# Gated linear attention on TensorE: one head per 32-row strip and PSUM bank in place of block-diagonal queries

## The chip, the cores and the metric

The program runs on one core of one Trainium2 chip, in one launch. The metric is the device time of an execution in microseconds (us). An engine is TensorE (PE, with its weight loads listed apart as PEld), VectorE (DVE), ScalarE (ACT), GpSimd (POOL) or SyncE (SP, which issues most transfers).

## The reference, cut to what matters

The program is a decoder trunk of two layers over 512 tokens. Each layer mixes three groups of heads, adds the result to the stream and runs a feed-forward network. The change touches one of the three groups, the gated linear attention with 4 heads of 32 key and 64 value channels:

```python
def step(state, inp):
    qc, kc, vc, gc = inp
    bcum = jnp.cumsum(gc, axis=2)
    o_inter = jnp.einsum('bhck,bhkv->bhcv', qc * jnp.exp(bcum), state)
    diff = bcum[:, :, :, None, :] - bcum[:, :, None, :, :]
    decay = jnp.exp(jnp.where(causal[None, None, :, :, None], diff, -jnp.inf))
    attn = jnp.einsum('bhik,bhjk,bhijk->bhij', qc, kc, decay)
    o_intra = jnp.einsum('bhij,bhjv->bhiv', attn, vc)
    ...
```

For each pair of a query i and an earlier key j in a chunk, the product of query and key is weighted in each of the 32 key channels by its own decay. The state carries the earlier chunks.

## The kernel before

Tokens stand in 4 chunks of 128. Channels of queries and keys stand on the 128 partitions: head h has partitions 32h to 32h+31 (`qkT[0]` queries, `qkT[1]` keys, 128 x 512 each).

The decay between i and j is split at a point between them, so that it becomes a factor of the query times a factor of the key. A chunk has 7 levels for this, with blocks of 64, 32, 16, 8, 4, 2 and 1 tokens (`LEVELS`). At each level, half of the chunk's tokens (64) act as queries and the other half as keys. The loop of lines 737 to 794 does for each chunk `t`:

- Lines 740 to 744: TensorE sums the log decays (`ghl` by the 0/1 matrix `tsel`) into PSUM in three pieces of 512, 512 and 128 columns. ScalarE takes the exponential into `E`, 9 planes of 128 tokens: one for each level, one for the state's update and one for its readout.
- Lines 745 to 747: ScalarE copies each head's queries into a block-diagonal tile `qbd`, whose other blocks are zero (line 730). The four heads lie side by side in its columns.
- Lines 751 to 762: VectorE multiplies `qbd` by each level's plane into `xq` (line 760, 4 heads x 64 queries = 256 columns, one instruction for each level). It multiplies four planes at a time by the keys (line 761), in place; these are the keys `xk`.
- Lines 764 to 765: VectorE writes the diagonal into `at`, the chunk's attention matrix.
- Lines 766 to 772: for each level, one matmul of all 128 rows: the weights are `xk` (128 x 128), 256 columns of `xq` stream past. Since `qbd` is zero outside of a head's own rows, each head's columns get its own product. VectorE then copies the allowed entries from PSUM into `at` under a mask (line 772). Two PSUM banks ("t") take turns.
- Lines 773 to 794: TensorE multiplies the state (line 777) and `at` (line 779) with their values into bank "o"; the keys are transposed (line 784), multiplied with the values (line 788) and added to the state `sbd`.

PSUM has 8 banks of 512 columns. The function `psum(tag)` (line 141) takes a tile of one bank from a pool with a fixed number for each tag: g 2, s 3, t 2, o 1. Which of a tag's banks a tile gets, and what it waits for, is settled by the planner of the language when it lays out the program. The planner also fixes the order of each engine's instructions, from its estimates of when each is ready and from the order in the source. So matmuls of the next projection, site "B" (line 834, through the helper `mm3` at lines 286 to 288, into banks "g"), stand between those of the loop in TensorE's queue. Each engine works through its queue in that order.

A matmul on float32 operands appears in the trace as two loads and two matmul records; a split operand (`hl`, `kt`, type fp32r) as one of each.

Of the kernel before, what the change touches and what calls it, by code (L numbers as in the profile page):

```python
# [10 lines left out]
F32 = mybir.dt.float32  # L11
# [5 lines left out]
ALU = mybir.AluOpType  # L17
AX = mybir.AxisListType

P = 128  # L20
# [11 lines left out]
GH = 4  # L32
DK = 32
# [10 lines left out]
XKP = ()  # L44
# [13 lines left out]
LEVELS = (64, 32, 16, 8, 4, 2, 1)  # L58
# [65 lines left out]
def trunk_kernel(ctx: ExitStack, tc: tile.TileContext, a, out):  # L124
    nc = tc.nc
# [6 lines left out]
    pp = ctx.enter_context(tc.tile_pool(name="pp", bufs=1, space=bass.MemoryType.PSUM))  # L132
    uid = [0]

    def nm(s):
        uid[0] += 1
        return f"{s}_{uid[0]}"

    PB = PBK

    def psum(tag):
        return pp.tile([P, 512], F32, tag=tag, name=nm("ps" + tag), bufs=PB[tag])

    def small(n, tag, bufs=4, dt=F32):
        return sm.tile([P, n], dt, tag=tag, name=nm(tag), bufs=bufs)
# [6 lines left out]
    o = 0  # L152
# [186 lines left out]
    with tc.tile_pool(name="x0", bufs=1, reuse_waits="tile") as xp:  # L339
# [8 lines left out]
        for t in range(NT):  # L348
            tk = slice(t * P, (t + 1) * P)
            r = xp.tile([P, D], F32, name=nm("xr"))  # L350
# [4 lines left out]
            for hf in range(2):  # L355
                m4 = slice(4 * hf, 4 * hf + 4)
                ps = psum("s")
# [90 lines left out]
    def mixer(l, norm, xkt, eu=None):  # L448
# [47 lines left out]
        with tc.tile_pool(name=f"mx{l}", bufs=1, reuse_waits="tile") as mp:  # L496
# [13 lines left out]
            with tc.tile_pool(name=f"ma{l}", bufs=1, reuse_waits="tile") as ap:  # L510
# [45 lines left out]
                for t in range(NT):  # L556
                    v = uv[:, t, 256:512]
                    nc.vector.tensor_scalar(v, v, vmean[:, t : t + 1], None, op0=ALU.subtract)
                    s = tmp(256)
# [5 lines left out]
                for t in range(NT):  # L565
                    v = uv[:, t, 256:512]
# [81 lines left out]
            with tc.tile_pool(name=f"mg{l}", bufs=1, reuse_waits="tile") as gp:  # L648
# [77 lines left out]
                nc.vector.tensor_copy(diag, dps[:, 0:16].rearrange("p (t h) -> p t h", t=NT))  # L726
                osb = mp.tile([P, NT, 256], F32, tag="PT", name=nm("osb"), bufs=3)
                sbd = gp.tile([P, 256], F32, name=nm("sbd"))
                qbd = gp.tile([P, GH, P], F32, name=nm("qbd"))
                nc.gpsimd.memset(qbd, 0.0)  # L730
                ats = []
                for n in range(2):
                    at_ = gp.tile([P, GH, P], F32, name=nm("at"))
# [3 lines left out]
                for t in range(NT):  # L737
                    tk = slice(t * P, (t + 1) * P)
                    E = gp.tile([P, 9, P], F32, tag="E", name=nm("E"), bufs=2)
                    for c0, c1 in ((0, 4), (4, 8), (8, 9)):  # L740
                        ps = psum("s")[:, 0 : (c1 - c0) * P]
                        nc.tensor.matmul(ps, ghl[:, 0, tk], tsel[:, c0 * P : c1 * P], start=True, stop=False)
                        nc.tensor.matmul(ps, ghl[:, 1, tk], tsel[:, c0 * P : c1 * P], start=False, stop=True)
                        nc.scalar.activation(E[:, c0:c1, :].rearrange("p l i -> p (l i)"), ps, AF.Exp, scale=1.0 / 16)
                    for h in range(GH):
                        r = slice(32 * h, 32 * h + 32)
                        nc.scalar.copy(qbd[r, h, :], qkT[0][r, tk])

                    xqs = []
                    xk = E[:, 0:8, :]  # L750
                    for l0, l1 in ((0, 4), (4, 8)):
                        for lv in range(l0, min(l1, 7)):
                            s = LEVELS[lv]
                            nb = 64 // s
                            xq = gp.tile([P, GH, 64], F32, tag="xq", name=nm("xq"), bufs=4)
                            xqs.append(xq)
                            ev = E[:, lv, :].rearrange("p (b u s) -> p b u s", u=2, s=s)[:, :, 1, :]
                            qv = qbd.rearrange("p h (b u s) -> p h b u s", u=2, s=s)[:, :, :, 1, :]
                            xv = xq.rearrange("p h (b s) -> p h b s", s=s)
                            nc.vector.tensor_tensor(xv, qv, ev.unsqueeze(1).to_broadcast([P, GH, nb, s]), op=ALU.mult)  # L760
                        (nc.gpsimd if l0 // 4 in XKP else nc.vector).tensor_tensor(xk[:, l0:l1], xk[:, l0:l1],
                                                qkT[1][:, tk].unsqueeze(1).to_broadcast([P, l1 - l0, P]), op=ALU.mult)
                    at = ats[t % 2]
                    nc.vector.copy_predicated(at, eye8.unsqueeze(1).to_broadcast([P, GH, P]),
                                              diag[:, t, :].unsqueeze(2).to_broadcast([P, GH, P]))
                    for lv, s in enumerate(LEVELS):
                        nb = 64 // s
                        ps = psum("t")[:, 0:256]
                        nc.tensor.matmul(ps, xk[:, lv, :], xqs[lv].rearrange("p h i -> p (h i)"), start=True, stop=True)
                        av = at.rearrange("p h (b u s) -> p h b u s", u=2, s=s)[:, :, :, 1, :]  # L770
                        mv = lmask[:, lv, :].rearrange("p (b s) -> p b s", s=s).unsqueeze(1).to_broadcast([P, GH, nb, s])
                        nc.vector.copy_predicated(av, mv, ps.rearrange("p (h b s) -> p h b s", h=GH, s=s))
                    ops = psum("o")[:, 0:256]
                    if t > 0:
                        xi = tmp(P)
# [4 lines left out]
                                         start=t == 0, stop=t == 0 or h == GH - 1)  # L780
                    nc.scalar.copy(osb[:, t, :], ops)
                    if t < NT - 1:
                        kps = psum("t")[:, 0:P]
                        nc.tensor.transpose(kps, xk[:, 7, :], ident)
                        ktok = tmp(P)
                        nc.scalar.copy(ktok, kps)
                        sps = psum("t")[:, 0:256]
                        nc.tensor.matmul(sps, ktok, gv[:, t, :], start=True, stop=True)
                        if t == 0:
                            nc.vector.tensor_tensor(sbd, sps, bdm, op=ALU.mult)  # L790
                        else:
                            sm_ = tmp(256)
                            nc.vector.tensor_tensor(sm_, sps, bdm, op=ALU.mult)
                            nc.vector.scalar_tensor_tensor(sbd, sbd, E[:, 8, 127:128], sm_, op0=ALU.mult, op1=ALU.add)
# [620 lines left out]
```

## Time and profile before

| what | us |
|---|---|
| median of 3 runs | 1343.45 |
| lowest and highest of them | 1343.28, 1351.97 |
| the profiled execution's own time | 1343.64 |
| its span, first to last instruction | 1341.9 |

The profiled execution lies 0.19 us above the median. Its time is 1.7 us more than its span. In the rows below, "x" is the number of instructions of a group, a duration is that of the record (matmul records overlap, since the engine starts one while the one before drains), and idle time follows with what ended it.

### The profile page before, as it was taken

To read this page: it belongs to the slowest core of one execution; us is meant where nothing else is said; L and a number is where in the kernel's file an instruction comes from. 1 tells how busy PE (TensorE), PEld (TensorE's weight loads), DVE (VectorE), ACT (ScalarE), POOL (GpSimd) and SP (SyncE) were. 2 spreads that over 40 slices of the span, in tenths; PEclk is the share of its full clock that TensorE was granted. 3 is DMA by queue.
4 is the path that set the end of the run, shared out by engine and by line. 5 is a ranking of instruction groups with operands and counts; after the bars stand their busy time and mean duration, and the time that the engine had idled before them with its cause. 6 is when DMAs were issued, how large, how long until landed. Compare 5 with 4: busy or idle time off the path is not lost.

```text
span 1341.9 us, 17478 instructions
## 1 busy us (share of the span) xinstructions
PE 1298.7 (97%) x6434; PEld 1054.7 (79%) x6434; DVE 949.1 (71%) x1661; ACT 624.5 (47%) x1164; POOL 176.4 (13%) x158
## 2 busy tenths in 40 slices
PE   6999999999999999999999999999999999999997
PEld 5888776777888888888888877767788888888785
DVE  5636889997865785586644498999778457736775
ACT  6344336665542543254442632667544435514532
POOL 2111021114000100010312102111220001000103
PEclk9999999999999999999999999999999999999999
DMA  8521131006335785384363302201343348754721
GB/s 280 156 81 48 32 95 32 17 17 159 109 99 121 206 213 152 105 203 111 96 181 97 91 21 63 79 17 33 91 129 95 110 120 205 225 126 126 195 88 64
DMA packets 128554, 150.41 MB, mean 112 GB/s; under 512 B 9034, under 2 KB 82516, under 8 KB 128468
## 3 DMA queue, kind: packets, MB, share of 16 engines
q1 hardware_dynamic: 115504, 128.31, 31.5%
q0 software_dynamic: 8704, 16.78, 7.4%
q10 hardware_dynamic: 4260, 4.20, 1.1%
q8 instruction: 51, 0.84, 0.3%
q14 instruction: 35, 0.29, 0.1%
HBM read 147.17 MB, written 2.10 MB: 111 GB/s over the span
## 4 chain that ended last, share of the span: by engine, by line
PE 77%; DVE 12%; ACT 4%; DMA 3%; issue 3%; POOL 1%; SPq 0%; ACTq 0%; DVEq 0%; POOLq 0%
PE psg L286 10%; PE psg L287 10%; PE psg L288 10%; PE pss L286 4%; PE pst L286 4%; PE pss L288 4%; PE pss L287 4%; PE pst L288 4%; PE pst L287 4%; PE pso L593 2%; DVE hl L274 2%; PE pst L1010 2%; PE pso L288 2%; PE pso L286 2%; PE pso L287 2%
## 5 line engine op out<-in xcount | busy, mean ns | idle before, releaser
L271 ACT CAST hl<-raw 128x1024 fp32r<-128x1024 f32 (+3 forms) x170 | 175.6, 1034 | 224.3 <-PE pst L288 66.2
L274 DVE TENSOR_TENSOR hl<-raw,hl 128x1024 fp32r<-128x1024 f32 (+3 forms) x170 | 207.8, 1223 | 100.3 <-ACT hl L271 97.5
L286 PE MATMUL psg<-hl,kt 128*128 128x512 f32 (+2 forms) x480 | 179.4, 375 | 4.1 <-ACT hl L271 2.1
L288 PE MATMUL psg<-hl,kt 128*128 128x512 f32 (+2 forms) x480 | 178.2, 372 | 0.0
L287 PE MATMUL psg<-hl,kt 128*128 128x512 f32 (+2 forms) x480 | 177.3, 370 | 0.0
L286 PEld LDWEIGHTS psg<-hl,kt 128*128 128x128 f32 x480 | 91.1, 190 | 19.0 <-DVE gqk L698 2.7
L288 PEld LDWEIGHTS psg<-hl,kt 128*128 128x128 f32 x480 | 91.1, 190 | 12.9
L287 PEld LDWEIGHTS psg<-hl,kt 128*128 128x128 f32 x480 | 91.0, 189 | 12.8
L287 PE MATMUL psg<-kt,hl 128*128 128x512 f32 x248 | 99.6, 402 | 1.2 <-DVE kt L249 1.2
L286 PE MATMUL psg<-kt,hl 128*128 128x512 f32 x248 | 99.6, 403 | 0.0
L288 PE MATMUL psg<-kt,hl 128*128 128x512 f32 x248 | 98.3, 398 | 0.0
L271 ACT CAST hl<-wx 128x1024 fp32r<-128x1024 f32 x48 | 50.3, 1049 | 78.6 <-PE pst L288 63.3
L274 DVE TENSOR_TENSOR hl<-wx,hl 128x1024 fp32r<-128x1024 f32 x48 | 58.7, 1223 | 18.0 <-ACT hl L271 17.4
L253 ACT CAST PT<-pst 128x384 fp32r<-128x384 f32 (+1 forms) x96 | 46.7, 519 | 37.9 <-PE pst L1010 37.6
L254 DVE TENSOR_TENSOR PT<-pst,PT 128x384 fp32r<-128x384 f32 (+1 forms) x96 | 54.8, 595 | 10.5 <-ACT PT L253 9.6
L1002 POOL TENSOR_TENSOR P<-P,rr 128x512 f32<-128x512 f32 x32 | 35.5, 1109 | 174.8 <-DVE rr L999 134.3
L1010 PE MATMUL pst<-ident,P 128*128 128x128 f32 x320 | 53.2, 277 | 2.6 <-DVE P L1004 2.6
L287 PEld LDWEIGHTS psg<-kt,hl 128*128 128x128 f32 x248 | 46.9, 189 | 9.9 <-DVE kt L249 2.0
L288 PEld LDWEIGHTS psg<-kt,hl 128*128 128x128 f32 x248 | 46.8, 189 | 8.0
L286 PEld LDWEIGHTS psg<-kt,hl 128*128 128x128 f32 x248 | 46.7, 189 | 7.8 <-ACT kt L253 0.3
L286 PE MATMUL pss<-hl,kt 128*128 128x512 f32 x128 | 50.3, 393 | 1.7 <-DVE ft L1302 1.3
L288 PE MATMUL pss<-hl,kt 128*128 128x512 f32 x128 | 50.0, 390 | 0.0
(442 smaller groups left out, 3139.6 us busy)
## 6 DMA issues: line engine op xcount, KB each, us to landing
raw<-in_w_gate_dram SPq DMA_DIRECT2D x44, 512.0 KB, 3.8
raw<-in_w_up_dram SPq DMA_DIRECT2D x44, 512.0 KB, 4.4
raw<-in_w_in_dram SPq DMA_DIRECT2D x32, 512.0 KB, 3.7
raw<-in_w_down_dram SPq DMA_DIRECT2D x20, 512.0 KB, 3.9
raw<-in_w_down_dram SPq DMA_DIRECT2D x36, 256.0 KB, 4.1
raw<-in_w_out_dram SPq DMA_DIRECT2D x16, 512.0 KB, 4.0
w<-in_cmp_w_k_dram SPq DMA_DIRECT2D x16, 256.0 KB, 5.4
w<-in_cmp_w_v_dram SPq DMA_DIRECT2D x16, 256.0 KB, 3.1
```

The lines of the kernel that those rows point to most:

```text
L253: nc.scalar.copy(hi, src)
L254: nc.vector.tensor_tensor(lo, src, hi.bitcast(F32), op=ALU.subtract)
L271: nc.scalar.copy(hl[:, 0, 0:n], raw[:, 0:n])
L274: e_.tensor_tensor(hl[:, 1, 0:n], raw[:, 0:n], hl[:, 0, 0:n].bitcast(F32), op=ALU.subtract)
L286: nc.tensor.matmul(ps, lh, rh, start=start, stop=False, skip_group_check=skip)
L287: nc.tensor.matmul(ps, lh, rl, start=False, stop=False, skip_group_check=skip)
L288: nc.tensor.matmul(ps, ll, rh, start=False, stop=stop, skip_group_check=skip)
L593: nc.tensor.matmul(ps[:, hh * 65 : (hh + 1) * 65], wu[:, kk, hh * P : (hh + 1) * P], kvS[w_i][:, s % 8, s // 8 : s // 8 + 65], start=s == ...
L1002: nc.gpsimd.tensor_tensor(ps_[i], ps_[i], rr[:, i : i + 1].to_broadcast([P, P * (i + 1)]), op=ALU.mult)
L1010: nc.tensor.transpose(T[:, c : c + P], ps_[i][:, j * P : (j + 1) * P], ident)
```

## The change

- All 8 PSUM banks become one tile, `banks`. `psum(tag)` gives a slice of it; a tag's banks are taken in turn, in the order of the source: g has banks 0 and 1, t 2 and 3, s 4 to 6, o 7.
- `qbd`, its clearing and its four copies for each chunk go. `xq` becomes one tile of 7 levels x 64 queries, and a level's query product has 64 columns in place of 256.
- A level's matmul becomes four, one for each head, on that head's 32 partitions, each with 64 columns into the head's own bank (2 to 5), at column 64 times the level. All 28 matmuls of a chunk come first in the source, then the seven masked copies, from the smallest block to the largest; a copy reads its level's columns of all four banks in one instruction.
- The sums of the log decays, the transposed keys and the state's product all use bank 6.

```diff
+    banks = pp.tile([P, 8, 512], F32, name="banks")
+    first_bank = {"g": 0, "t": 2, "s": 4, "o": 7}
+    taken = {k: 0 for k in first_bank}
     def psum(tag):
-        return pp.tile([P, 512], F32, tag=tag, name=nm("ps" + tag), bufs=PB[tag])
+        taken[tag] += 1
+        return banks[:, first_bank[tag] + (taken[tag] - 1) % PB[tag], :]
...
-                qbd = gp.tile([P, GH, P], F32, name=nm("qbd"))
-                nc.gpsimd.memset(qbd, 0.0)
...
                     for c0, c1 in ((0, 4), (4, 8), (8, 9)):
-                        ps = psum("s")[:, 0 : (c1 - c0) * P]
+                        ps = banks[:, 6, 0 : (c1 - c0) * P]
...
-                    for h in range(GH):
-                        r = slice(32 * h, 32 * h + 32)
-                        nc.scalar.copy(qbd[r, h, :], qkT[0][r, tk])
+                    xq = gp.tile([P, 7, 64], F32, tag="xq", name=nm("xq"), bufs=2)
...
-                            xq = gp.tile([P, GH, 64], F32, tag="xq", name=nm("xq"), bufs=4)
-                            nc.vector.tensor_tensor(xv, qv, ev.unsqueeze(1).to_broadcast([P, GH, nb, s]), op=ALU.mult)
+                            ev, qv = (v.rearrange("p (b u s) -> p b u s", u=2, s=s)[:, :, 1, :] for v in (E[:, lv, :], qkT[0][:, tk]))
+                            nc.vector.tensor_tensor(xq[:, lv, :].rearrange("p (b s) -> p b s", s=s), qv, ev, op=ALU.mult)
...
-                    for lv, s in enumerate(LEVELS):
+                    for lv in range(7):
+                        for h in range(GH):
+                            r = slice(DK * h, DK * h + DK)
+                            nc.tensor.matmul(banks[:, 2 + h, lv * 64 : lv * 64 + 64], xk[r, lv, :], xq[r, lv, :], start=True, stop=True)
+                    for lv in reversed(range(7)):
+                        s = LEVELS[lv]
                         nb = 64 // s
-                        ps = psum("t")[:, 0:256]
-                        nc.tensor.matmul(ps, xk[:, lv, :], xqs[lv].rearrange("p h i -> p (h i)"), start=True, stop=True)
+                        ps = banks[:, 2 : 2 + GH, lv * 64 : lv * 64 + 64]
...
-                        nc.vector.copy_predicated(av, mv, ps.rearrange("p (h b s) -> p h b s", h=GH, s=s))
+                        nc.vector.copy_predicated(av, mv, ps.rearrange("p h (b s) -> p h b s", s=s))
...
-                        kps = psum("t")[:, 0:P]
+                        kps = banks[:, 6, 0:P]
...
-                        sps = psum("t")[:, 0:256]
+                        sps = banks[:, 6, 0:256]
```

## Rows read from the trace of the kernel before

**Rows 1.** The page: the span, and each engine's busy time, share and instructions.

```profile
span 1341.9 us, 17478 instructions
PE 1298.7 (97%) x6434; PEld 1054.7 (79%) x6434; DVE 949.1 (71%) x1661; ACT 624.5 (47%) x1164; POOL 176.4 (13%) x158
```

**Rows 2.** Busy time by stretch: the loop over chunks in layer 0 and layer 1.

```profile
core 0: us, PE busy (x) PEld busy (x) DVE busy (x) ACT busy (x) POOL busy (x), PEclk, DMA share, GB/s
118.70:156.00 37.30, 36.73 (x167) 27.16 (x166) 33.21 (x86) 9.38 (x28) 1.59 (x2) 1.00 0.03 12
774.00:811.00 37.00, 36.43 (x165) 27.28 (x165) 32.83 (x86) 9.37 (x28) 1.59 (x2) 1.00 0.02 9
```

**Rows 3.** Groups by line, TensorE, 118.7 to 156: busy us, mean ns | idle.

```profile
L769 PE MATMUL pst<-xq,E 128*128 128x256 f32 x56 | 16.2, 395 | 0.4 <-DVE E L761 0.3
L286 PE MATMUL psg<-hl,kt 128*128 128x512 f32 x22 | 10.3, 469 | 0.1
L288 PE MATMUL psg<-hl,kt 128*128 128x512 f32 x22 | 9.8, 446 | 0.0
L287 PE MATMUL psg<-hl,kt 128*128 128x512 f32 x22 | 9.5, 430 | 0.0
L779 PE MATMUL pso<-gv,at 128*128 128x64 f32 x24 | 3.1, 272 | 0.1
L788 PE MATMUL pst<-gv,tmp 128*128 128x256 f32 x6 | 2.0, 423 | 0.0
L777 PE MATMUL pso<-sbd,tmp 128*128 128x256 f32 x6 | 1.9, 392 | 0.0
```

**Rows 4.** Timeline of TensorE, start and us: the first and last of nine matmuls.

```profile
95.31 0.39 PE L286 MATMUL psg<-kt,hl 128*128 128x512 f32 x1
...
97.12 0.39 PE L288 MATMUL psg<-kt,hl 128*128 128x512 f32 x1
```

**Rows 5.** Timeline of TensorE's weight loads: full arrays, 256 and 64 columns streamed.

```profile
792.14 0.85 PEld L769 LDWEIGHTS pst<-xq,E 128*128 128x128 f32 x4
...
126.48 0.97 PEld L779 LDWEIGHTS pso<-gv,at 128*128 128x128 f32 x8 [0.52 <-DVE at L772]
```

**Rows 6.** Timeline of TensorE around matmuls that use 17 rows of the array.

```profile
90.83 0.39 PE L287 MATMUL psg<-kt,hl 128*128 128x512 f32 x1
91.14 0.96 PEld L684 LDWEIGHTS pss<-wup,tmp 17*128 17x128 f32 x8 [0.35 <-issue]
...
92.23 0.50 PE L288 MATMUL psg<-kt,hl 128*128 128x512 f32 x1
...
92.57 0.40 PE L286 MATMUL psg<-kt,hl 128*128 128x512 f32 x1
```

**Rows 7.** Groups by line, VectorE, 118.7 to 156.

```profile
L772 DVE COPY_PREDICATED at<-m,pst 128x256 f32<-128x256 uint8 x27 | 13.7, 506 | 0.7 <-PE pst L769 0.5
L760 DVE TENSOR_TENSOR xq<-qbd,E 128x256 f32<-128x256 f32 x24 | 10.3, 430 | 3.1 <-PE pst L769 2.6
L761 DVE TENSOR_TENSOR E<-E,gqk 128x512 f32<-128x512 f32 x8 | 5.5, 685 | 0.1
...
L825 DVE SCALAR_TENSOR_TENSOR tmp<-psg,rstd,cf 128x64 f32<-128x64 f32 x4 | 1.1, 271 | 0.0
...
L776 DVE TENSOR_TENSOR tmp<-E,gqk 128x128 f32<-128x128 f32 x3 | 0.8, 280 | 0.0
```

**Rows 8.** Groups by line, ScalarE, 118.7 to 156.

```profile
L747 ACT COPY qbd<-gqk 32x128 f32<-32x128 f32 x12 | 3.6, 296 | 9.8 <-DVE xq L760 9.6
L744 ACT ACTIVATE E<-pss 128x512 f32<-128x512 f32 x4 | 2.2, 598 | 0.1
```

More of the change, by code (lines that the diff above doesn't have):

```diff
@@ L744, in mixer @@
                         nc.scalar.activation(E[:, c0:c1, :].rearrange("p l i -> p (l i)"), ps, AF.Exp, scale=1.0 / 16)
-                    for h in range(GH):
-                        r = slice(32 * h, 32 * h + 32)
-                        nc.scalar.copy(qbd[r, h, :], qkT[0][r, tk])
-                    xqs = []
+                    xq = gp.tile([P, 7, 64], F32, tag="xq", name=nm("xq"), bufs=2)
                     xk = E[:, 0:8, :]
@@ L753, in mixer @@
                             s = LEVELS[lv]
-                            nb = 64 // s
-                            xq = gp.tile([P, GH, 64], F32, tag="xq", name=nm("xq"), bufs=4)
[L756 to L759, printed above, removed]
-                            nc.vector.tensor_tensor(xv, qv, ev.unsqueeze(1).to_broadcast([P, GH, nb, s]), op=ALU.mult)
-                        (nc.gpsimd if l0 // 4 in XKP else nc.vector).tensor_tensor(xk[:, l0:l1], xk[:, l0:l1],
+                            ev, qv = (v.rearrange("p (b u s) -> p b u s", u=2, s=s)[:, :, 1, :] for v in (E[:, lv, :], qkT[0][:, tk]))
+                            nc.vector.tensor_tensor(xq[:, lv, :].rearrange("p (b s) -> p b s", s=s), qv, ev, op=ALU.mult)
+                        nc.vector.tensor_tensor(xk[:, l0:l1], xk[:, l0:l1],
                                                 qkT[1][:, tk].unsqueeze(1).to_broadcast([P, l1 - l0, P]), op=ALU.mult)
```

## The prediction

> **What bounds the kernel now.** I read the page first: TensorE is busy for 97% of the span, every other engine for 71% or less [rows 1]. That would make TensorE's own work the price of everything. But the busy time counts records that stretch over waits, so I took the stretch in which the chunk loop runs and summed its work by hand. There TensorE shows 36.73 us of 37.30, VectorE 33.21 (89%), and the second layer repeats it within 0.3 us, at full granted clock [rows 2].
>
> What a record really costs is the distance between starts. Nine 512-column matmuls of the projection lie 1.81 us apart from first to last: 0.226 each [rows 4]. The level matmuls start (0.85-0.19)/3 = 0.22 apart, and those with 64 columns (0.97-0.19)/7 = 0.111 [rows 5]. In the stretch [rows 3] that is 56 x 0.22 = 12.3 us for the levels (14 records a chunk), 66 x 0.226 = 14.9 for projection B, 24 x 0.111 = 2.7 for line 779 and 12 x 0.22 = 2.6 for lines 777 and 788. The other 9 of the 167 records are wide or narrow; at 0.11 to 0.226 they are 1.0 to 2.0, I take 1.5. Sum 34.0. So TensorE loses 3.3 us of 37.3 in a layer, 6.6 in both, to waits in its fixed order. The loop stands between two limits that lie close together: TensorE's work at 91%, VectorE's at 89%. A change that takes load from VectorE alone can give back 6.6 us and no more; the rest must come from TensorE's own work.
>
> **The change, part by part** (both layers, 8 chunks).
>
> *The levels on TensorE.* Removed: 8 x 14 = 112 records at 0.22, 24.6 us. Added: 8 x 28 matmuls in two records each, 448 records with 64 streamed columns and a load of 128 columns on 32 rows. The nearest full-array row has the same 64 columns and costs 0.111 [rows 5]. The nearest row on a part of the array is line 684 with 17 rows: its eight loads also start (0.96-0.19)/7 = 0.11 apart [rows 6], so fewer rows alone buy nothing. But all eight use the same rows; no row shows loads on different strips in succession. Upper end: every load waits for the one before, 448 x 0.111 = 49.7 us, 25.1 more than now. Lower end: four strips load at the same time, 49.7/4 = 12.4, 12.2 less than now. I take one exposed step for each matmul: of its two records the second must follow the first on the same strip, like line 684, while the first lies under the head before it. That is 224 x 0.111 = 24.9: +0.3 us. It is nearer to line 684 than the lower end is, and it uses strips as far as an engine that starts matmuls in order can.
>
> Line 684's loads take no less time on 17 rows than the others on 128. The Trainium skill says why that is to be expected (TensorE: Matmul & The Clock Gate, "LDWEIGHTS (loading the stationary operand)"): the load's time goes by its columns, not its rows. The trace agrees, and by that rule alone, with loads in a row, the sum would end at the upper end, which is the slow rival below.
>
> *Going into strips and back.* From the start of the full-array matmul at 90.83 to that at 92.57 lie 1.74 us [rows 6]. The work between is 2 x 0.226 + 8 x 0.111 = 1.34. So a visit to a part of the array cost 0.40 (a wait for data may hide in it). One visit a chunk: 8 x 0.40 = +3.2 us. Ends: 0, if TensorE would have waited at that place anyway, and 6.4, if projection matmuls stand inside of each block of 28.
>
> *VectorE.* The query products shrink from 256 to 64 columns. 256 columns take 0.430, 128 take 0.280 (line 776) [rows 7]; the line through both gives 0.205 for 64, and the 64-column line 825, which also reads PSUM, 0.271. At 0.205, 7 x 8 x 0.225 = 12.6 us of VectorE go. The masked copies (506 ns), the key products and the diagonal keep their sizes. VectorE is not alone in setting the pace, so this only helps through TensorE's lost 6.6 us. The seven query products no longer share four buffers with the matmuls (line 760 waited 2.6 us for line 769), and seven hand-overs from VectorE to TensorE become one for a chunk. In return all copies wait for the whole block, and the next block for all copies. Ends: nothing, and all 6.6. I take -6: the copies leave 7 x 0.506 = 3.5 us a chunk in which TensorE has projection matmuls to run (66 in the stretch), and while the block runs VectorE has the next chunk's products.
>
> *ScalarE and POOL.* 32 copies at 0.296 [rows 8] and two clearings go. ScalarE is busy 9.4 us of 37.3 [rows 2]: nothing.
>
> *One bank for the sums.* Three pieces through one bank: the second and third wait for an exponential of 0.598 [rows 8]. Price if uncovered 2 x 0.6 x 8 = 9.6 us. I take nothing: `E` has two buffers, so a chunk's sums are made while the chunk before runs, and B's matmuls cover them. The cover is gone if B is late.
>
> *Fixed banks elsewhere.* A tag's banks now turn in the order of the source. With the same count of banks and waits on the same readers I take nothing, but the planner's order may move anywhere: 3 us either way.
>
> **Sum:** +0.3 + 3.2 - 6 = -2.5. From the profiled execution's 1343.64 that is 1341.1; its time stands 0.19 above the median, so I say 1341. That is 0.2%, and a change of under 1% (13.4 us) I count as none that can be told here. The forecast is no change. Its own range is 1335 to 1348, for records spaced at 0.042 to 0.07 us (448 x 0.042 = 18.8, -5.8 + 3.2 - 6 = -8.6; 448 x 0.07 = 31.4, +6.8 + 3.2 - 6 = +4.0).
>
> **The rivals.**
>
> *Strips really run side by side.* Four loads at once: 12.4 us of levels, -12.2 + 3.2 - 6 = -15.0: 1328.6. For it speaks that head and bank change with each matmul, so neither the weights nor the results collide. Against it, the two records of one head follow each other in order. The gain passes 1% once a record costs under 0.031 us: 448 x 0.031 = 13.9. The Trainium skill has this as its rule (TensorEngine Tiling (Array Packing), "Key Properties"): strips take weights and matmuls independently of each other. No row of before shows two strips.
>
> *Strips take turns.* The change then does not do what it says: 448 records at 0.111, +25.1 + 3.2 - 6.6 = +21.7: 1365. TensorE is then the only limit, a chunk's block takes 6.2 us in place of 3.1, and all lost time is filled. For it speaks that the one row on part of the array is not faster than a full one; against it, that row never changes strip. It passes 1% from 0.091 us for a record (448 x 0.091 = 40.8, +16.2 + 3.2 - 6).
>
> *A chain through the block.* Block, seven copies, next block: 3.1 + 0.4 + 3.5 = 7.0 us and two hand-overs, against 37.3/4 = 9.3 for a chunk now. It does not bind unless the block takes 5.5; if hand-overs and projection work inserted between made it bind all the same, the gain of 6 goes: 1347, still no change. That lies in the forecast's range.
>
> The same page of the skill also speaks against the change in its "Key Properties": a change of tiling mode drains TensorE. The trace agrees as far as line 684 shows it, with the 0.40 us above.
>
> **How the numbers follow.** Forecast with its chain case 0.50 (0.44 within 1%, 0.04 faster, 0.02 slower), side by side 0.24 (0.20 faster, 0.04 within), taking turns 0.24 (0.21 slower, 0.03 within), the planner's order alone 0.02 (slower). Faster 0.24, within 1% 0.51, slower 0.25. The range goes from 1327, just under the first rival's value, to 1360, which leaves out the upper half of the second rival's chance (0.12) and the lower part of the first's (0.07).
>
> **What would show it.** Starts of loads in the changed loop: 0.055 apart on average if I am right, 0.028 if strips run side by side, 0.11 if they take turns. The block of 56 records in one piece, 3.1 us long, with some 0.4 lost around it. VectorE's busy time in the stretch down by about 6 us a layer, the query products near 0.2. Waits of the masked copies on the block, at most one for a chunk. TensorE's lost time in the stretch, counted as above, near 0.5 us a layer. I am wrong if the load spacing is outside 0.031 to 0.091, if the waits around bank 6 show up on TensorE, or if time moves in stretches far from the loop.

## The result, and the profile after

The changed kernel takes 1334.29 us (median of 20 runs, 1329.50 to 1355.94), the kernel before 1348.11 us beside it (20 runs, 1342.66 to 1363.45). The ratio is 0.991, 95% interval [0.9891, 0.9929]: 0.9% faster, within the 1% that the forecast called no change, though the interval reaches past it on the fast side. Runs more than 1.5% above the fastest of their kernel (four of the 20 after, one of the 20 before) stay out of the ratio; the means over all runs, 1338.9 and 1348.3, have the ratio 0.993. In a later comparison the ratio was 0.9909 [0.9879, 0.9938]. The profiled execution took 1332.43 us, 11.2 less than the one before.

The page after, which answers to [rows 1]:

```profile
span 1330.6 us, 18010 instructions
PE 1291.7 (97%) x6770; PEld 1053.7 (79%) x6770; DVE 938.5 (71%) x1661; ACT 617.2 (46%) x1132; POOL 175.2 (13%) x156
```

TensorE has 336 records more and is busy 7.0 us less; VectorE is busy 10.6 us less. To see where the time left, I cut both traces at the same matmuls of the projections (counted from zero, the groups of three 125 and 175 on TensorE for the loop of layer 0, 870 and 925 for layer 1). The loops took 62.4 and 63.6 us before, 58.0 and 57.9 after: 10.1 of the 11.2 us. Every other stretch moved by 1.5 us or less. Busy time of these two stretches, columns as in [rows 2]; the kernel before:

```profile
111.10:173.50 62.40, 61.43 (x287) 47.37 (x286) 55.40 (x131) 21.37 (x48) 7.65 (x8) 1.00 0.18 51
763.50:827.00 63.50, 62.53 (x302) 48.73 (x301) 54.47 (x130) 22.34 (x50) 6.85 (x8) 1.00 0.17 49
```

and after:

```profile
110.90:168.90 58.00, 57.73 (x453) 45.86 (x453) 49.19 (x126) 17.78 (x35) 7.86 (x8) 0.97 0.20 56
759.60:817.60 58.00, 57.48 (x469) 46.27 (x468) 48.37 (x125) 18.74 (x37) 7.14 (x8) 1.00 0.19 55
```

VectorE is busy 6.2 and 6.1 us less in them, as the prediction had it. TensorE fills the stretches to 99%, and to 98% before, so its busy time does not tell work from waiting; the starts of its records do. Its weight loads in the loop, timeline after (start and us; the row that answers to [rows 5]):

```profile
127.77 0.76 PEld L765 LDWEIGHTS banks<-xq,E 32*128 32x128 f32 x24 [0.31 <-DVE E L756]
...
135.44 1.72 PEld L765 LDWEIGHTS banks<-xq,E 32*128 32x128 f32 x56 [0.25 <-issue]
...
143.59 0.98 PEld L765 LDWEIGHTS banks<-xq,E 32*128 32x128 f32 x32 [0.25 <-DVE E L756]
```

A load here lasts 0.19 us, so the 56 loads of a chunk start (1.72 - 0.19)/55 = 0.028 us apart. The single records behind the last row show how: loads at 143.587, .593, .600 and .607, then at 143.695, .702, .708 and .715. Four start within 20 ns, and the sets stand about 0.11 us apart. That is the time between two loads in [rows 5], now paid once for four strips. What the Trainium skill states as a rule (TensorEngine Tiling (Array Packing), "Key Properties": strips take weights and matmuls independently) the trace bears out.

Groups by line, TensorE and VectorE, 112.6 to 149.8 after, beside [rows 3] and [rows 7]:

```profile
L765 PE MATMUL banks<-xq,E 32*128 32x64 f32 x224 | 9.2, 285 | 0.3 <-DVE E L756 0.2
L292 PE MATMUL banks<-hl,kt 128*128 128x512 f32 x21 | 9.1, 435 | 0.0
L779 PE MATMUL banks<-gv,at 128*128 128x64 f32 x24 | 3.1, 272 | 0.0
```

```profile
L772 DVE COPY_PREDICATED at<-m,banks 128x256 f32<-128x256 uint8 x23 | 12.4, 538 | 4.2 <-PE banks L765 3.9
L756 DVE TENSOR_TENSOR E<-E,gqk 128x512 f32<-128x512 f32 x7 | 4.8, 684 | 0.1
L755 DVE TENSOR_TENSOR xq<-gqk,E 128x64 f32<-128x64 f32 x24 | 4.1, 220 | 0.7 <-ACT E L747 0.7
```

A query product fell from 430 to 220 ns. The copies now wait 3.9 us for the block (0.5 for line 769 before), as they must when seven levels come in one piece; TensorE has projection matmuls meanwhile.

Going into the strips and leaving them is what costs. Timeline of TensorE after, around two blocks:

```profile
143.59 1.12 PE L765 MATMUL banks<-xq,E 32*128 32x64 f32 x32
144.64 0.70 PE L777 MATMUL banks<-sbd,tmp 128*128 128x256 f32 x2
...
146.00 0.90 PE L765 MATMUL banks<-xq,E 32*128 32x64 f32 x24
146.82 0.50 PE L292 MATMUL banks<-hl,kt 128*128 128x512 f32 x1
147.16 0.39 PE L293 MATMUL banks<-hl,kt 128*128 128x512 f32 x1
147.38 0.39 PE L291 MATMUL banks<-hl,kt 128*128 128x512 f32 x1
```

From the last strip's start to the next full-array matmul lie 0.200 us in place of 0.028; the one after follows in 0.33 in place of 0.227; and the first set of four is followed in 0.140 in place of 0.112. Together that is 0.17 + 0.11 + 0.03 = 0.31 us. The way in comes on top. Timeline of TensorE after, ahead of the first block:

```profile
112.26 0.40 PE L746 MATMUL banks<-tsel,ghl 128*128 128x512 f32 x1
112.59 0.66 PE L765 MATMUL banks<-xq,E 32*128 32x64 f32 x10
```

The block starts 0.33 us after a 512-column matmul, though the profile shows no wait there, where the next full-array matmul would start after 0.23: 0.09 more, about 0.40 us for a visit. The planner parted blocks (line 765 comes in pieces of 10, 22, 24, 32 and 56), so there are 14 visits in the two loops, not 8. Summed over the 14, the steps around the blocks are 5.7 us longer than the same steps elsewhere; up to 0.8 us of that is waiting for data.

### The profile page after: what moved, and what is told of

It reads as the page before. It is cut to its first block, busy times and chain, and to the rows that moved or that the text cites. A ratio compares the mean times of both kernels' runs of the same rounds, so it can differ in the third digit from the quotient of the medians.

```text
span 1330.6 us, 18010 instructions
## 1 busy us (share of the span) xinstructions
PE 1291.7 (97%) x6770; PEld 1053.7 (79%) x6770; DVE 938.5 (71%) x1661; ACT 617.2 (46%) x1132; POOL 175.2 (13%) x156
## 5 line engine op out<-in xcount | busy, mean ns | idle before, releaser
L291 PE MATMUL banks<-hl,kt 128*128 128x512 f32 (+2 forms) x704 | 264.6, 376 | 4.3 <-ACT hl L276 1.9
L293 PE MATMUL banks<-hl,kt 128*128 128x512 f32 (+2 forms) x704 | 265.0, 377 | 0.0
L292 PE MATMUL banks<-hl,kt 128*128 128x512 f32 (+2 forms) x704 | 264.3, 376 | 0.0
L291 PEld LDWEIGHTS banks<-hl,kt 128*128 128x128 f32 x704 | 133.2, 189 | 28.8 <-ACT hl L276 2.2
L292 PE MATMUL banks<-kt,hl 128*128 128x512 f32 x384 | 152.5, 397 | 0.0
L291 PE MATMUL banks<-kt,hl 128*128 128x512 f32 x384 | 152.0, 398 | 0.0
L293 PE MATMUL banks<-kt,hl 128*128 128x512 f32 x384 | 150.9, 394 | 0.0
L293 PEld LDWEIGHTS banks<-hl,kt 128*128 128x128 f32 x704 | 133.2, 189 | 22.4
L292 PEld LDWEIGHTS banks<-hl,kt 128*128 128x128 f32 x704 | 133.1, 189 | 22.4 <-DVE hl L279 0.3
L293 PEld LDWEIGHTS banks<-kt,hl 128*128 128x128 f32 x384 | 72.3, 188 | 13.4
L292 PEld LDWEIGHTS banks<-kt,hl 128*128 128x128 f32 x384 | 72.5, 189 | 13.0 <-DVE kt L259 0.4
L291 PEld LDWEIGHTS banks<-kt,hl 128*128 128x128 f32 x384 | 72.3, 189 | 13.0 <-ACT kt L258 0.3
L292 PE MATMUL banks<-act,hl 128*128 128x512 f32 x176 | 68.7, 390 | 0.6 <-DVE act L259 0.6
L293 PE MATMUL banks<-act,hl 128*128 128x512 f32 x176 | 69.1, 392 | 0.0
L258 ACT CAST PT<-banks 128x384 fp32r<-128x384 f32 (+1 forms) x96 | 47.3, 518 | 46.5 <-PE banks L1010 45.2
L291 PE MATMUL banks<-act,hl 128*128 128x512 f32 x176 | 68.8, 394 | 0.0
L388 DVE TENSOR_TENSOR xT<-xT,banks 128x512 f32<-128x512 f32 x56 | 37.5, 681 | 43.0 <-PE banks L293 43.0
L259 DVE TENSOR_TENSOR PT<-banks,PT 128x384 fp32r<-128x384 f32 (+1 forms) x96 | 55.3, 598 | 12.1 <-ACT PT L258 10.7
```

What stands on the lines that cost most here:

```text
L258: nc.scalar.copy(hi, src)
L259: nc.vector.tensor_tensor(lo, src, hi.bitcast(F32), op=ALU.subtract)
L291: nc.tensor.matmul(ps, lh, rh, start=start, stop=False, skip_group_check=skip)
L292: nc.tensor.matmul(ps, lh, rl, start=False, stop=False, skip_group_check=skip)
L293: nc.tensor.matmul(ps, ll, rh, start=False, stop=stop, skip_group_check=skip)
L388: nc.vector.tensor_tensor(xT[:, m, :], xT[:, m, :], ps, op=ALU.add)
```

## The theories

**S**: strips at work at the same time shorten TensorE's work, and the loops follow TensorE. **V**: the loops follow VectorE, and the gain is its narrower products. **P**: fixed banks, or another order from the planner, made the difference. In what follows "the loops" are the two stretches above, 126.0 us before and 115.9 after; a sentence that the order is the same means that TensorE's matmuls stand in one sequence in both traces.

Two readings are given: the measured time with its ratio, and the loops of the profiled execution. A third helps where the clock differs. The time of each run goes with its mean granted clock: a line through the 20 runs of the changed kernel gives 12.7 us for 0.01. The last column reduces the mean time to a clock of 1 by that line, an estimate, and too low where something other than the clock sets the pace (heads outside and one block are left out for that). The first three looks at the changed kernel's order differ by 2 us in this column, so smaller differences in it mean nothing.

| kernel | median us | mean clock | loops us | reduced us |
|---|---|---|---|---|
| before (60 runs) | 1345 to 1347 | 0.994 to 0.996 | 126.0 | 1341 |
| changed | 1334.29 | 0.991 | 115.9 | 1328 |
| changed, again | 1334.54 | 0.993 | 116.0 | 1327 |
| changed, two tiny matmuls more | 1335.35 | 0.993 | 117.1 | 1326 |
| two strips at a time | 1341.68 | 0.987 | 121.9 | 1330 |
| levels in turn | 1350.29 | 0.992 | 129.9 | 1339 |
| wide products, changed kernel | 1343.37 | 0.988 | 128.2 | 1332 |
| narrow products, kernel before | 1346.89 | 0.991 | (other work in them) | 1337 |
| key products on GpSimd | 1347.14 | 0.986 | 125.0 | 1329 |
| fixed banks, kernel before | 1348.43 | 0.988 | 123.3 | 1334 |

## Experiments on the strips

**Heads outside, levels inside.** The order of all other instructions is the same.

```diff
-for lv in range(7):
-    for h in range(GH):
+for h in range(GH):
+    for lv in range(7):
```

> The changed kernel, with the 28 matmuls of a chunk ordered by head and then level, so that seven matmuls in a row use the same 32 rows; nothing else moves. Theory S (the gain is TensorE's: loads on four strips start together, so 56 records take 1.6 us and not 3.1): on one strip each load follows the one before at 0.11 us, a block takes 56 x 0.112 = 6.3 us, 4.7 more in 8 chunks: +30 to +38 us over the changed kernel, 1362 to 1372. Theory V (the gain is VectorE's, whose query products shrink by 12.6 us; the block lies under other work): the longer block stays hidden, 0 to +8. Theory P (fixed banks and the planner's new order): 0.

Measured: 1375.18 us, ratio to before 1.0219 [1.0173, 1.0264]; loops 75.9 and 77.0. The weight loads of one block:

```profile
133.53 5.39 PEld L765 LDWEIGHTS banks<-xq,E 32*128 32x128 f32 x56
```

(5.39 - 0.19)/55 = 0.095 us apart on average, but the single records show three spacings. The first five start at 133.535, .643, .752, .865 and .976, 0.11 apart: the levels of one head use the same strip and load in turn. Then the records of two strips interleave, some 0.055 apart. The last ones, at 1.2 GHz, stand 0.213 apart. The steps from one strip record to the next sum to 38.8 us in both loops, against 14.6: +24.2. The loops grew by 37.0. The clock has a part in both: 149 of the 434 steps, 19.0 us, lie at 1.2 GHz; the others average 0.070 us, at which all 434 would take 30 us, some 16 more than in the changed kernel. Busy time by stretch, the clock in the third column from the end:

```profile
126.00:134.00 8.00, 8.00 (x57) 6.22 (x58) 5.95 (x17) 2.11 (x5) 0.00 (x0) 1.00 0.00 1
134.00:142.00 8.00, 8.00 (x62) 7.18 (x62) 2.84 (x6) 0.27 (x1) 0.00 (x0) 0.58 0.01 2
```

Before the block TensorE ran at 2.4 GHz, from within it on mostly at 1.2, and the loops average 0.82. Without strips side by side the change would have been a loss.

**Two strips at a time.** Heads 0 and 1 in turn over the levels, then 2 and 3; the order of all else is the same.

```diff
-for lv in range(7):
-    for h in range(GH):
+for lv, h in [(lv, h) for hp in (0, 2) for lv in range(7) for h in (hp, hp + 1)]:
```

> The changed kernel with a chunk's 28 matmuls in another order: heads 0 and 1 in turn over the seven levels, then heads 2 and 3, so that two strips are at work and not four; every other instruction stays in its place. Theory S: records 0.056 us apart in place of 0.028, 12.5 us of TensorE's time more in both loops together, so loops of 63 to 66 us, and 1342 to 1350. Theory V (VectorE sets the pace of the loops): no more than 4 us over the changed kernel. If the engine can overlap strips only in sets of four, the records stand 0.1 apart and the time is that of the order by heads, about 1375.

Measured: 1341.68 us, ratio 0.9959 [0.9928, 0.999]; loops 60.4 and 61.5. Its weight loads:

```profile
144.67 1.48 PEld L765 LDWEIGHTS banks<-xq,E 32*128 32x128 f32 x32 [0.24 <-DVE E L756]
```

That is (1.48 - 0.19)/31 = 0.042 apart, less than the 0.056 that I worked out. The single records show sets of two, 0.105 to 0.112 apart, and around the change from heads 0 and 1 to heads 2 and 3 two such series run at once: the later heads' first loads, at 145.176 and .182, start before the earlier heads' loads at 145.221, .332 and .444. So a strip waits for its own earlier record only, not for all that stand before it in the queue. The steps between strip records sum to 20.7 us, 6.1 over the changed kernel's 14.6, and the loops took 121.9, 6.0 over its 115.9. A part of both is the clock, 0.97 in both loops here and in one of the changed kernel's. The kernel with two tiny matmuls more has the same order and 0.97 in both: against it the steps are 5.6 us longer (15.1 there) and the loops 4.7 (117.1). What TensorE's work grows by, the loops grow by, but for 0.5 us of gaps that it fills: S, and against V alone.

The same run limits S. The levels before took 112 records at 0.215 us, 24.1 us. Here the strips' steps and the 14 visits (5.1 us) take TensorE some 26, 2 more than that, and still the loops are 4.1 us shorter than the 126.0 of the kernel before (0.9 of it is a pair of sums a layer that now lies ahead of the stretch). So a part of the whole change's gain does not come from strips side by side.

**Levels in turn.** Each level's four strips stand right before its copy, as in the kernel before.

```diff
-for lv in range(7):          # all 28 matmuls
-    ...
-for lv in reversed(range(7)):  # then all copies
+for lv in reversed(range(7)):
+    for h in range(GH): ...  # four matmuls
+    ...                      # then this level's copy
```

> The changed kernel, with each level's four matmuls followed by its masked copy, level after level, in the same four banks, so that a level's matmuls wait for the copy before. TensorE then enters and leaves the strips seven times a chunk instead of once or twice. Theory S with its cost of a visit (0.2 to 0.4 us): some 40 to 48 more visits, +10 to +20 us, and more if the waits for the copies are not covered. If visits cost nothing and the waits are covered by projection matmuls: -2 to +4.

Measured: 1350.29 us, ratio 1.0022 [0.9994, 1.005]; loops 64.4 and 65.5, granted clock 1.00 in both. The planner put other work between the levels:

```profile
132.37 0.45 PE L765 MATMUL banks<-xq,E 32*128 32x64 f32 x8
132.75 0.50 PE L292 MATMUL banks<-hl,kt 128*128 128x512 f32 x1
133.09 0.43 PE L745 MATMUL banks<-tsel,ghl 128*128 128x512 f32 x1
...
134.52 0.45 PE L765 MATMUL banks<-xq,E 32*128 32x64 f32 x8
135.06 0.70 PE L776 MATMUL banks<-sbd,tmp 128*128 128x256 f32 x2
```

56 visits in place of 14: 42 x 0.40 = 16.8 us. The strips' own steps are some 3 us less, mostly because no piece leaves a set of four incomplete, and the loops are 14.0 longer. Gaps between TensorE's records grew too, from 0.8 to 3.5 us in both loops, so waits for the copies have a part in it. Strips side by side bring nothing here, because the visits take it. The gain needs a chunk's levels to stay together.

**A visit alone.** 32 small matmuls a layer, ahead of the loops, once on the full array and once on 32 of its rows.

```diff
+if wsite[0] == "gr":
+    nc.tensor.matmul(banks[:, 7, 0:4], identb[0:k, :], identb[0:k, 0:4], ...)  # k = 128 | 32
```

> The changed kernel with one more small matmul (4 columns, all 128 rows, a constant as both operands, result not used) after each group of three in the projection before the loop (site gr, 64 places in both layers). It is the measure for the next run: some 0.06 to 0.11 us at each place, 4 to 7 us in all.

> The same small matmul on the first 32 rows alone. Its excess over the run on 128 rows is the price of going into a strip and back by itself, with no data to wait for. If a visit costs the 0.40 us of the prediction: 64 x 0.3 to 0.4, 19 to 26 us more. If visits cost nothing: 0.

One run each: 1352.98 and 1352.48 us. The two have one order, but it departs from the changed kernel's in more than 200 places, so these times say nothing about a visit. The rows do. The planner put the 32 small matmuls of layer 0 in a row, and 21 of those of layer 1; the other 11 of layer 1 stand alone between projection matmuls of 256 columns, and each is a visit. Timeline of TensorE around one such group of three, full array first, then 32 rows:

```profile
768.61 0.18 PE L478 MATMUL banks<-mb 128*128 128x4 bf16 x1
768.65 0.36 PE L291 MATMUL banks<-hl,kt 128*128 128x256 f32 x1
...
769.09 0.18 PE L478 MATMUL banks<-mb 128*128 128x4 bf16 x1
```

```profile
768.54 0.17 PE L478 MATMUL banks<-mb 32*128 32x4 bf16 x1
768.64 0.38 PE L291 MATMUL banks<-hl,kt 128*128 128x256 f32 x1
...
769.20 0.17 PE L478 MATMUL banks<-mb 32*128 32x4 bf16 x1
```

From one small matmul to the next lie 0.48 us with the full array and 0.65 to 0.66 with 32 rows, in all ten groups. A visit costs 0.17 us there, with one short bf16 matmul, against 0.40 in the loop, with fp32 ones.

**A chunk in one block.** The key products in one instruction over all levels, so that nothing parts the 28 matmuls.

```diff
-for l0, l1 in ((0, 4), (4, 8)):
+for l0, l1 in ((0, 8),):
```

> The changed kernel with the key products of a chunk in one instruction over all eight levels, so that a chunk's 28 matmuls become ready together and the planner has no reason to part them. If a change from full arrays to strips and back costs about 0.35 us, as the kernel with its levels in turn showed, and a chunk saves half a visit to one: 1.5 to 3 us less than the changed kernel, loops of 56.5 to 57.5 us. Rival (TensorE waits for the longer product): loops of 59 to 62 us. Rival O (the planner's order decides): anything from 5 us less to 12 us more, with waits in places that have nothing to do with the block.

Measured: 1366.06 us, ratio 1.0135 [1.0087, 1.0184]; loops 68.2 and 68.1. It has 8 visits, and pays for them in waits; the planner's order departs from the changed kernel's in some 50 places. Waits of TensorE's weight loads, 110 to 180 (us in total, times, longest):

```profile
PEld banks L745 <- ACT E L747: 4.6, 4, 1.4
PEld banks L765 <- DVE E L756: 3.3, 3, 2.0
PEld banks L788 <- ACT tmp L786: 1.6, 3, 1.0
PEld banks L745 <- DVE tmp L793: 1.6, 2, 1.2
```

TensorE stood still for 5.5 us of each loop (gaps between its records; 0.3 and 0.5 in the changed kernel), in part at the sums, behind bank 6. That is 10 us of the 20.4 by which the loops grew. The clock took part too: it averaged 0.85 and 0.87 in these loops (0.97 and 1.00 in the changed kernel). Six visits fewer, 2.4 us, did not pay for the later start of the first 16 matmuls; how much of the loss is the later start, how much the order and how much the clock is not separated here.

## Experiments on VectorE, GpSimd and the banks

**Narrow products in the kernel before.** Three heads' query products are left out, so the outputs differ; instructions and matmuls keep their number and size.

```diff
-nc.vector.tensor_tensor(xv, qv, ev.unsqueeze(1).to_broadcast([P, GH, nb, s]), ...)
+nc.vector.tensor_tensor(xv[:, 0], qv[:, 0], ev, ...)   # xq: four cleared buffers
```

> The kernel before, full-array matmuls and block-diagonal queries, with VectorE's query products made for the first head's 64 columns alone (the other heads' stay zero, so three heads' products are left out). This is VectorE's relief of 12 us by itself. Theory W (after the wide products lost all of the gain: VectorE alone paces the loop): -9 to -13 us against the kernel before. Theory B (both engines stand near their limit, TensorE loses only 6.6 us of the two loops, so VectorE's relief alone can give back no more than that): -3 to -7.

Measured: 1346.89 us, ratio 1.0001 [0.9963, 1.0038]. Query products in the whole run, the kernel before and then this one:

```profile
L760 DVE TENSOR_TENSOR xq<-qbd,E 128x256 f32<-128x256 f32 x56 | 23.5, 428 | 6.2 <-PE pst L769 5.3
```

```profile
L765 DVE TENSOR_TENSOR xq<-qbd,E 128x64 f32<-128x64 f32 x56 | 10.2, 218 | 1.4 <-PE pst L774 1.3
```

13.3 us less for VectorE, and no change in the measured time; reduced to one clock it is about 4 us. Narrower products alone do not make the gain of 13 (reduced) that the whole change makes: V falls as its sole cause. In this profile the granted clock was 0.50 from 60 to 90 us, far ahead of the loops, and the planner moved other work into them, so the loops are not compared.

**Wide products in the changed kernel.**

```diff
-nc.vector.tensor_tensor(xq[:, lv, :]..., qv, ev, op=ALU.mult)                  # 64 columns
+nc.vector.tensor_tensor(xq..., qv.unsqueeze(1)..., ev.unsqueeze(1)..., ...)    # 4 x 64, all used rows the same
```

> The changed kernel, with VectorE's 56 query products widened back to 256 columns (each head's queries written four times, one quarter used), so that VectorE has its 12 us back and TensorE's matmuls stay. Theory S: +0 to +3 us over the changed kernel. Theory V: +9 to +13, nearly all of the gain lost.

Measured: 1343.37 us, ratio 0.9993 [0.9962, 1.0024]: most of the gain is gone, about 4 us of it at one clock. The loops took 64.9 and 63.3 us, 12.3 more than the changed kernel's. About 24 projection matmuls in them ran 0.2 us longer at 1.2 GHz, some 4.8 us. Most of the rest are waits, which the kernel before and the changed one don't have at this size. TensorE's waits, 110 to 170:

```profile
PE banks L745 <- DVE tmp L797: 1.2, 1, 1.2
PE banks L745 <- ACT E L747: 0.7, 1, 0.7
PE banks L769 <- DVE E L760: 0.6, 1, 0.6
PE banks L781 <- DVE tmp L780: 0.3, 1, 0.3
```

TensorE's gaps are 3.0 and 3.5 us, against 0.3 and 0.5. Strips with wide products leave the loops where the fixed banks alone have them (128.2 less 4.8 of clock, and 123.3). (The changed kernel has six such slow matmuls itself, 1.3 us.) So neither half does it as far as it was run alone: before, TensorE hid VectorE's load; once the block is short, VectorE is next in line, and the narrow products keep it out of the way. S is not sufficient. The planner's order differs from the changed kernel's in some 30 places, so how much of the waits is the products' own and how much the order's stays open.

One kernel was not run: fixed banks and narrow products with the matmuls on the full array. Reduced to one clock, the two by themselves come to 7 and 4 us of the 13 of the whole change, so much of the gain might be had without strips. Not all of it: with each kind of matmul at its median step, TensorE's records in the loops before add up to 117.4 us, or 116.5 without the pair of sums a layer that the changed kernel makes ahead of the stretch. The changed kernel takes 115.9, or 114.7 at 2.4 GHz throughout. So 0.6 to 1.8 us at the least need the strips, and for the rest their share is not shown.

**Half of the key products on GpSimd.**

```diff
-nc.vector.tensor_tensor(xk[:, l0:l1], ...)
+(nc.gpsimd if l0 == 4 else nc.vector).tensor_tensor(xk[:, l0:l1], ...)
```

> The changed kernel, with the key products of the last four planes of each chunk on GpSimd in place of VectorE: 8 x 0.68 us less on VectorE. Theory W (VectorE paces the changed loop too): -3 to -5 us against the changed kernel. Theory B after the change (TensorE's work, some 85% of the loop, and the chain block, copies, block set the rest): -2 to 0. If GpSimd's product, some 1.3 us, comes on the path into the block: +2 to +8.

Measured: 1347.14 us, ratio 0.9999 [0.9969, 1.0029]; loops 62.6 and 62.4. The wait that does it, 110 to 180, and the product behind it, a group by line:

```profile
PE banks L765 <- POOL E L756: 3.0, 4, 1.5
```

```profile
L756 POOL TENSOR_TENSOR E<-E,gqk 128x512 f32<-128x512 f32 x4 | 5.8, 1450 | 26.1 <-ACT E L747 15.3 <-ACT osb L781 8.5 <-DVE xq L755 2.3
```

1.45 us on GpSimd in place of 0.68 on VectorE: the strips of the last three levels wait for it. What VectorE was relieved of, TensorE waits for. Beside these waits the clock took part (0.95 and 0.97 in the loops), and the order differs in some 20 places; at one clock the loss is 1 to 2 us, no more than repeats of the changed kernel differ by.

**Fixed banks only**, in the kernel before. The planner's order changes with them: TensorE's matmuls differ from the kernel before's in more than 100 places, the first of them a chunk's sums that come earlier.

```diff
-return pp.tile([P, 512], F32, tag=tag, name=nm("ps" + tag), bufs=PB[tag])
+taken[tag] += 1
+return banks[:, first_bank[tag] + (taken[tag] - 1) % PB[tag], :]
```

> The kernel before, with only the eight PSUM banks made one tile whose banks are taken in the order of the source; block-diagonal queries and full-array matmuls stay. Theories S and V: -3 to +3 us against the kernel before. Theory P: most of the 12 us gained.

Measured: 1348.43 us, ratio 1.0023 [0.9996, 1.0051]; loops 61.1 and 62.2. By the measured time P gives nothing. The loops are 2.7 us shorter, and at one clock the whole would be some 7 us faster. Chance hardly explains the lower clock: it is 0.983 to 0.993 in all ten runs, and 0.994 or more in 23 of the 26 runs of the kernel before beside them. In the loops it is 1.00, so it falls elsewhere. Why, and where the other 4 us would come from, stays open.

**The changed kernel with two tiny matmuls more, and once more as it is.** The first gives the planner a reason to find another order. (Its expectation says four matmuls; the trace has two, one in each layer.)

```diff
+if wsite[0] == "gr" and n == 0 and t == 0:
+    nc.tensor.matmul(banks[:, 7, 0:4], identb, identb[:, 0:4], start=True, stop=True)
```

> The changed kernel with four matmuls of 4 columns added in the projection ahead of the loops (0.1 us of work in all), which lets the planner lay out the program anew. Theory S: within 3 us of the changed kernel, loops of 58 us. Rival O (much of the gain is the order that the planner happened to find): 5 to 15 us slower than the changed kernel, loops of 60 to 63 us, with the same spacing of the strips.

> The changed kernel once more, for a second profile. Theory S (the gain is TensorE's time in the two loops): the loops take 58 us each again (57 to 59.5 where the granted clock stays at 2.4 GHz there), and the time is 1327 to 1336. Rival L (the 58.0 and 57.9 us were one favourable execution): loops of 60 us or more at the same granted clock. If the granted clock falls to 1.2 GHz inside the loops again, the fall belongs to the strips; if it falls elsewhere only, it does not.

Measured: 1335.35 us, ratio 0.9917 [0.9884, 0.995], and 1334.54 us, 0.9909 [0.9879, 0.9938]. The planner kept its order but for the added matmuls, so the first is a third look at one order and no test of rival O. The loops took 58.0 and 59.1, and 56.8 and 59.2 us: 117.1 and 116.0 together. The gain repeats (L falls). The excess of single loops is the clock, which fell at 116.5 us in the profile of after and at 769 in the repeat, each time in the projection matmuls behind the first chunk's strips. Busy time by stretch, after and then the repeat:

```profile
116.00:116.50 0.50, 0.50 (x3) 0.41 (x3) 0.50 (x1) 0.28 (x1) 0.00 (x0) 1.00 1.01 393
116.50:117.00 0.50, 0.50 (x2) 0.36 (x2) 0.50 (x4) 0.00 (x0) 0.00 (x0) 0.51 0.60 229
...
120.00:120.50 0.50, 0.50 (x18) 0.43 (x14) 0.00 (x0) 0.00 (x0) 0.00 (x0) 1.00 0.00 0
```

```profile
769.00:772.00 3.00, 3.00 (x9) 2.28 (x7) 1.93 (x6) 0.00 (x0) 0.00 (x0) 0.53 0.67 206
```

## Why the prediction was right in time and wrong in mechanism

The time, 1334 against 1341 forecast, lies in the range, and the call of no change holds by a tenth of a per cent of the ratio. That is luck in good part. The forecast change was -2.5 us; it is -11.2 between the two profiles and -13.8 between the medians. The time lies just under 1335 to 1348, the range of the forecast's own mechanism, and a spacing of 0.028 lies outside of the 0.031 to 0.091 that the prediction named as its sign of being wrong. The mechanism is that of the first rival, strips side by side, and the time stayed in the range only because the visits went the other way.

**The levels on TensorE: wrong.** The step that failed is "one exposed step for each matmul: of its two records the second must follow the first on the same strip ... while the first lies under the head before it". The second record does follow the first on its strip, but it holds up no other strip. 448 records at 0.028 are 12.5 us, against 112 at 0.215 (steps in the trace of before), 24.1: -11.6, near the lower end that I had named, -12.2. In the trace the blocks take 15.0, since the pieces of 10 and 22 records are not whole sets of four: -9.1 in place of +0.3. That one row on 17 rows of the array [rows 6] was nearest was no ground to go to the middle: it could not show two strips. Its rule, that a load's time goes by its columns (the Trainium skill, TensorE: Matmul & The Clock Gate, "LDWEIGHTS (loading the stationary operand)"), holds within a strip, as the first five records of heads outside show, 0.11 apart on 32 rows.

**Visits: the price was right, the count was not.** 0.40 from [rows 6], and 0.40 in the loop. But I counted 8 and there are 14, 5.7 us in place of 3.2, within the upper end of 6.4 that I gave for projection work between the strips.

**VectorE's -6: right in size.** The products cost 220 ns (205 assumed), and VectorE is 6 us a layer lighter. From start to start, the loops have -9.1 for the levels, +5.7 for the visits and -0.9 for a pair of sums a layer that now lies ahead of the stretch (4 x 0.235). They are 10.1 shorter, so all else gave 5.8, with some 1 us of clock against it. About 1.4 us of lost time a loop is left by the same count (4.3 before), not the 0.5 that I named. "Can give back 6.6 us and no more" holds for VectorE alone (0 measured, 4 at one clock). That the 5.8 is VectorE's relief is not shown: fixed banks alone took 2.7 us off the loops, and fewer hand-overs and fewer changes between kinds of matmul are in it too. What was wrong is the use of the term: I let the relief fill lost time beside a block that stayed as long as it was. With a shorter block, most of it went into keeping up with TensorE: take it away and the loops grow by 12.3 - 4.8 = 7.5 us, or about 1 more if the changed kernel's own slow matmuls are taken off too.

**One bank for the sums: right.** No wait of a matmul itself for a sum's bank is in the loop of layer 0; its loads wait 1.7 us. All of those, 110 to 170, after (before, line 742 waited 0.8 us for line 744):

```profile
PEld banks L745 <- DVE tmp L793: 0.7, 2, 0.4
PEld banks L745 <- ACT E L747: 0.6, 3, 0.2
PEld banks L745 <- DVE sbd L790: 0.4, 1, 0.4
```

The kernels with wide products and with one block show that the cover is thin: there the same waits reach TensorE.

**Fixed banks:** no difference in the measured time alone (1.0023), and more than the 3 us that I allowed if the reduced time is believed. **A chain through the block** did not bind: 1.5 us lie between a block's first and last start, not the 5.5 from which it would. **ScalarE and POOL: right**, nothing.

**The first rival's own price**, -15.0, was too much: the blocks of strips gave 9.1 and not 12.2, and the visits cost 5.7 and not 3.2. Its 1328.6 lies 5.7 us under the measured median for another reason too: it starts from 1343.64, and the kernel before had a median of 1348.11 in the runs beside the changed one.

## What to carry to other kernels

Four 32-row strips with their own banks cost TensorE about a quarter of the same matmuls in turn, but only if successive matmuls go to different strips and the work stays together: each visit took back 0.4 us, and 56 visits took back everything. When a row of the trace cannot show the thing in dispute, keep the price at both ends and let the chances say so, rather than settle in the middle. And where two engines stand at 91% and 89% of a loop, price their reliefs together: each alone measured as nothing here, and both as 0.9%.

## What was not expected of the hardware

- A strip's records pass those of other strips that stand earlier in the queue; for strips, TensorE does not work through its queue in order. With two strips at a time the next two began before the first were done (0.042 us a record, where strict sets of two would give 0.056).
- The granted clock fell to 1.2 GHz inside the loops in kernels with long strip blocks: on average 0.97 and 1.00 in the changed kernel, 0.97 and 0.97 with two strips at a time, 0.92 and 0.97 with wide products, 0.85 and 0.87 with one block, 0.82 and 0.82 with heads outside. It stayed at 1.00 there in the kernel before, with fixed banks only, and with strips in pieces of 8 records. At the lower clock 512-column matmuls start 0.427 us apart in place of 0.227. What sets it off is open; it also fell far from the loops, in kernels with and without strips.
- Of the changed kernel's 20 runs, those with a mean granted clock of 0.997 or 0.998 took 1329.5 to 1333.1 us, those at 0.978 to 0.980 took 1351.6 to 1355.9. A difference of 0.5% between two kernels is as large as one of 0.005 in that clock.
